# Moving the weight buffers by 96 bytes against the activations, and two split transfers joined

## The chip, the cores and the metric

The kernel runs on one core of a Trainium2 chip. The metric is the device time of one execution in microseconds (us), the median of three runs. One further execution was recorded by the hardware profiler; all rows below come from it. The engines are named as the profile names them: PE (TensorE, matrix multiplication), PEld (the loading of PE's stationary operand, which overlaps PE), DVE (VectorE), ACT (ScalarE), POOL (GpSimd) and SP (SyncE, which here only issues transfers). SPq and ACTq are the issues of transfers from SP and ACT.

## What is computed

One decoder layer for 256 tokens of width 1024, in float32: two token mixers side by side (attention with 8 heads, and a causal pooling mixer), each gated, then a feed-forward part with a causal convolution of width 3. Cut to what matters here:

```python
h = rmsnorm(x, norm_mix_g)
q, k, v, u_pool, gate_logits = split(h @ w_in)       # 1024 x 4096
attn = attention(rotary(rmsnorm(q)), rotary(rmsnorm(k)), v)
pooled = multiscale_pool_mixer(u_pool, w_pool, pool_scale)
gates = sigmoid(gate_logits + b_gate)
x = x + (gates[0] * (attn @ w_branch_attn) + gates[1] * (pooled @ w_branch_pool)) @ w_out
up = causal_depthwise_conv(rmsnorm(x, norm_ffn_g) @ w_up, conv_w, conv_b)
gate, val = split(up)                                # 2 x 2816 columns
return x + (silu(gate) * val) @ w_down
```

## The kernel before

Everything is kept transposed: channels on the 128 partitions, the 256 tokens along the row. Every product is made of three passes of PE in the type fp32r: each operand is cut into a high part (ACT copies it into fp32r: `high`, L80) and a low part (DVE subtracts the high part from the original: `low`, L84), and `mm3` (L92 to L94) adds high x high, high x low and low x high into one PSUM bank. Each of those passes first loads a stationary operand of 128x128 and then streams a moving operand. From the pooling input on (`feature_tile`, `branch`, `tile_part`, `down`), the weights are the stationary operand and 256 columns of activations move. In the stage of q, k and v (`project`, L283) it is the other way round: the activations are stationary and 512 columns of weights move.

Weights come in blocks of 128x2048 through three pools of four buffers each: `raw` (as loaded, by `load`, L121, from SP's queue), `whi` and `wlo` (high and low parts). In a partition's row of SBUF the order is: the small tiles of the pool `const`, then `raw`, `whi`, `wlo`, then the pool `act` with the activations, whose first tile is `xq` (the input x and the weights of q, interleaved by blocks of 128 channels), then `xhi`, `xlo` and the later activations. In the built program `raw`, `whi` and `wlo` start at bytes 24000, 56768 and 89536 of the row, `xq` at 122304 and `xhi` at 146912. Buffers and steps inside them are multiples of 512 bytes, so, modulo 512, all weight operands of PE stand at 448 and all activations of the dense stages at 480.

The order on each engine is the order of the program. SP issues the blocks of `xq` (L190 to L199: two of 128 channels each, then three of 256), the first weights of k, the table `par` of vectors (L202), and then a weight block each time a buffer comes free. The first block of `xq` goes out in two pieces: x of that block and the norm weights from SP (L196), the weights of q from ACT (L195). The first matmul needs `xhi` of block 0 (DVE, L226) and the high part of q's weights (ACT, L80). At the end eight output tiles are added to x by DVE (L703) and sent out, seven by SP (L705); the eighth goes in two halves of 64 partitions, one from SP and one from ACT (L707).

Of the kernel before, what the change touches and what calls it, by code (L numbers as in the profile page):

```python
# [8 lines left out]
F32 = mybir.dt.float32  # L9
# [5 lines left out]
P = 128  # L15
S = 256
NT = S // P
D = 1024
KD = D // P
H = 8  # L20
DH = 64
AW = H * DH
# [30 lines left out]
FFN_AHEAD = 6  # L53
KREADY = 0
FIRST = 2
XCUTS = (1, 2, 4, 6, 8)


@with_exitstack
def hybrid_layer_kernel(ctx: ExitStack, tc: tile.TileContext, xq_d, par_d, wkv_d, wpg_d,  # L60
                        wpool_d, wba_d, wbp_d, wout_d, wup_d, wdn_d, out_d):
    nc = tc.nc

    const = ctx.enter_context(tc.tile_pool(name="const", bufs=1))
# [3 lines left out]
    act = ctx.enter_context(tc.tile_pool(name="act", bufs=1))  # L68
# [109 lines left out]
    nc.vector.memset(ones, 1.0)  # L178


    xq_all = act.tile([P, KD + KD * (S + AW)], F32, name="xq")
    gmix = xq_all[:, 0:KD]
    xq = xq_all[:, KD:].rearrange("p (k c) -> p k c", c=S + AW)
    xT = xq[:, :, 0:S]
# [5 lines left out]
    cut = 0  # L190
    for k in XCUTS:
        end = KD + k * (S + AW)
        if k == 1:

            nc.scalar.dma_start(out=xq_all[:, KD + S:end], in_=xq_d[:, KD + S:end])  # L195
            nc.sync.dma_start(out=xq_all[:, 0:KD + S], in_=xq_d[:, 0:KD + S])  # L196
        else:
            nc.sync.dma_start(out=xq_all[:, cut:end], in_=xq_d[:, cut:end])
        cut = end  # L199
    nc.scalar.activation(scrap, ones[:, 0:1], AF.Copy)  # L200
    load(2)
# [8 lines left out]

    ident = const.tile([P, P], F32, name="ident")
    make_identity(nc, ident)
    mhalf = const.tile([P, H], F32, name="mhalf")
    nc.gpsimd.memset(mhalf, -0.5)
    mask = const.tile([P, 3, P], F32, name="mask")
# [215 lines left out]
    def scores(hp):  # L431
        ps = ps2.tile([P, 2, 512], F32, tag="ps2", name=f"ps_s{hp}")
        for j in range(2):
            rows = slice(j * DH, (j + 1) * DH)
            nc.tensor.matmul(ps[:, j, P:3 * P], qT[rows, hp, P:S], kT[rows, hp, :], start=True, stop=True)
            nc.tensor.matmul(ps[:, j, 0:P], qT[rows, hp, 0:P], kT[rows, hp, 0:P], start=True, stop=True)
        sm = tmp.tile([P, 2, 3 * P], F32, tag="big", bufs=4, name=f"sm{hp}")
        nc.vector.tensor_tensor(sm, ps[:, :, 0:3 * P],
                                mask.rearrange("p a b -> p (a b)")[:, None, :].to_broadcast([P, 2, 3 * P]), ALU.add)
        mx = tmp.tile([P, 2, 2], F32, tag="mx", name=f"mx{hp}")  # L440
        for t in (1, 0):
            nc.vector.tensor_reduce(mx[:, t, :], sm[:, :, TOK[t]], axis=AX.X, op=ALU.max)
        nc.vector.tensor_scalar(mx, mx, -(DH ** -0.5), None, op0=ALU.mult)
        sums = tmp.tile([P, 2, 2], F32, tag="sums", name=f"sums{hp}")
        for j in range(2):
            for t in (1, 0):
                nc.scalar.activation(sm[:, j, TOK[t]], sm[:, j, TOK[t]], AF.Exp, bias=mx[:, t, j:j + 1],
                                     scale=DH ** -0.5, accum_out=sums[:, t, j:j + 1])
        rs = tmp.tile([P, 2, 2], F32, tag="rs", name=f"rs{hp}")
        nc.vector.reciprocal(rs, sums)  # L450
        for t in (1, 0):
            n = TOK[t].stop - TOK[t].start
            nc.gpsimd.tensor_tensor(sm[:, :, TOK[t]], sm[:, :, TOK[t]],
                                    rs[:, t, :, None].to_broadcast([P, 2, n]), ALU.mult)
        later(4, weigh, hp, sm)
# [46 lines left out]
    for n in range(2 * KD):  # L502
        if n >= FIRST and (n - FIRST) % 4 == 0:
            scores((n - FIRST) // 4)
        if n == 10:
# [126 lines left out]
    def down(i, ms):  # L632
        if i % 2 == 0 and i // 2 not in wd:
            wd[i // 2] = chunk("dn")
        hi, lo = wd[i // 2]
        for m in ms:
            sl = slice((i % 2) * D + m * P, (i % 2) * D + (m + 1) * P)
            o = acc[m // 2][:, (m % 2) * S:(m % 2 + 1) * S]
            first = i == 0 and m % 2 == 0
            nc.tensor.matmul(o, hi[:, sl], acch[i], start=first, stop=False, skip_group_check=True)  # L640
            nc.tensor.matmul(o, hi[:, sl], accl[i], start=False, stop=False, skip_group_check=True)  # L641
            nc.tensor.matmul(o, lo[:, sl], acch[i], start=False, stop=i == KF - 1, skip_group_check=True)  # L642
        if i % 2 == 1 and len(ms) == KD:
            spent.add(next(c for c in his if his[c] is hi))
# [54 lines left out]
    for m in (0, 2, 4, 6, 1, 3, 5, 7):  # L699
        for i in (KF - 2, KF - 1):  # L700
            down(i, (m,))
        o = acc[m // 2][:, (m % 2) * S:(m % 2 + 1) * S]
        nc.vector.tensor_tensor(xT[:, m, :], o, xT[:, m, :], ALU.add)  # L703
        if m < 7:
            nc.sync.dma_start(out=out_d[:, m, :], in_=xT[:, m, :])  # L705
    for q, rows in ((nc.sync, slice(0, P // 2)), (nc.scalar, slice(P // 2, P))):
        q.dma_start(out=out_d[rows, 7, :], in_=xT[rows, 7, :])  # L707


    last = {}  # L710
# [70 lines left out]
```

## Time and profile before

| | us |
|---|---|
| median of three runs | 347.86 (347.85 to 348.05) |
| the profiled execution, whole | 347.8 |
| its span, first to last instruction | 346.0 |
| PE busy in the span | 340.3 (98%) |
| PEld, DVE, ACT, POOL busy | 329.3, 259.3, 198.1, 89.4 |
| mean rate of all transfers | 181 GB/s |

Busy times of matmuls overlap: a matmul is recorded from its start to the modelled end of its result, while the next has already begun. The pace of PE is therefore read from the distance between starts, not from the duration of one. The granted clock of PE is 1.00 of its 2.4 GHz level in every slice of the span but the last, after the last matmul.

### The profile page before, as it was taken

The numbers are of one execution on the slowest core, as the hardware profiler recorded it, in microseconds if no ns is written. First come the engines' busy times: TensorE is split into PE (matmuls) and PEld (weight loads), VectorE is DVE, ScalarE is ACT, GpSimd is POOL, SyncE is SP. The second block draws the span as 40 slices with busy tenths as digits, with TensorE's granted clock in tenths as the row PEclk, the third lists the DMA queues.
The fourth block names the chain that finished last, engine by engine and source line by source line (L and its number), as shares of the span: only waits on it lengthen the run. The fifth ranks groups of instructions, "written<-read, shape, count | busy, mean of one in ns | idle before, by whom it ended". The sixth has DMA issues, their size and how long they took to land.

```text
span 346.0 us, 6726 instructions
## 1 busy us (share of the span) xinstructions
PE 340.3 (98%) x2736; PEld 329.3 (95%) x2736; DVE 259.3 (75%) x411; ACT 198.1 (57%) x319; POOL 89.4 (26%) x103
## 2 busy tenths in 40 slices
PE   8999999999999999999999999999999999999995
PEld 7887899999999999999999999999999999999995
DVE  4969889787587585798699977777777777768633
ACT  4956534634748944776467755555556464646420
POOL 1007991112202034123142212121212121221230
PEclk9999999999999999999999999999999999999999
DMA  7985642365272560574257557364646455641003
GB/s 273 421 333 211 217 168 108 150 214 213 86 265 90 230 215 30 172 275 170 116 197 268 183 206 243 122 244 131 236 137 228 145 223 168 209 180 54 0 2 121
DMA packets 10414, 62.76 MB, mean 181 GB/s; under 512 B 1168, under 2 KB 2448, under 8 KB 3472
## 3 DMA queue, kind: packets, MB, share of 16 engines
q1 hardware_dynamic: 10160, 62.01, 49.9%
q8 instruction: 21, 0.34, 0.4%
q10 hardware_dynamic: 224, 0.33, 0.3%
q14 instruction: 9, 0.07, 0.1%
HBM read 61.29 MB, written 1.05 MB: 180 GB/s over the span
## 4 chain that ended last, share of the span: by engine, by line
PE 90%; DMA 5%; DVE 3%; ACT 1%; issue 0%; POOL 0%; SPq 0%; ACTq 0%
PE ps_up L94 12%; PE ps_up L92 12%; PE ps_up L93 12%; PE ps_d L642 6%; PE ps_d L641 6%; PE ps_d L640 6%; PE ps_g L92 5%; PE ps_g L94 4%; PE ps_g L93 4%; DMA raw_k<-in_wkv 3%; PE ps_v L283 3%; PE ps_out L92 2%; PE ps_out L94 2%; PE ps_out L93 2%; PE ps_bp L92 1%; DMA xq<-in_xq 1%
## 5 line engine op out<-in xcount | busy, mean ns | idle before, releaser
L92 PE MATMUL ps_up<-hhi,hi_up 128*128 128x256 f32 x352 | 98.5, 280 | 0.0
L94 PE MATMUL ps_up<-hhi,lo_up 128*128 128x256 f32 x352 | 98.4, 279 | 0.0
L93 PE MATMUL ps_up<-hlo,hi_up 128*128 128x256 f32 x352 | 98.3, 279 | 0.0
L94 PEld LDWEIGHTS ps_up<-hhi,lo_up 128*128 128x128 f32 x352 | 66.2, 188 | 0.2 <-DVE lo_up L84 0.2
L92 PEld LDWEIGHTS ps_up<-hhi,hi_up 128*128 128x128 f32 x352 | 66.2, 188 | 0.0
L93 PEld LDWEIGHTS ps_up<-hlo,hi_up 128*128 128x128 f32 x352 | 66.2, 188 | 0.0
L84 DVE TENSOR_TENSOR lo_up<-raw_up,hi_up 128x1024 fp32r<-128x1024 f32 x44 | 54.5, 1242 | 6.1 <-ACT hi_up L80 6.1
L641 PE MATMUL ps_d<-al,hi_dn 128*128 128x256 f32 x176 | 49.1, 279 | 0.0
L640 PE MATMUL ps_d<-ah,hi_dn 128*128 128x256 f32 x176 | 49.1, 279 | 0.0
L642 PE MATMUL ps_d<-ah,lo_dn 128*128 128x256 f32 x176 | 49.1, 279 | 0.0
L623 POOL TENSOR_TENSOR c_v<-c_g,c_v 128x256 f32<-128x256 f32 x22 | 16.2, 736 | 121.4 <-DVE c_v L606 121.4
L80 ACT ACTIVATE hi_up<-raw_up 128x1024 fp32r<-128x1024 f32 x44 | 44.9, 1044 | 0.0
L92 PE MATMUL ps_g<-xhi,hi_g 128*128 128x256 f32 x128 | 36.5, 285 | 0.0
L93 PE MATMUL ps_g<-xlo,hi_g 128*128 128x256 f32 x128 | 35.7, 279 | 0.0
L94 PE MATMUL ps_g<-xhi,lo_g 128*128 128x256 f32 x128 | 35.7, 279 | 0.0
L80 ACT ACTIVATE ah<-c_v 128x256 fp32r<-128x256 f32 x22 | 9.2, 419 | 45.7 <-POOL c_v L623 45.7
L641 PEld LDWEIGHTS ps_d<-al,hi_dn 128*128 128x128 f32 x176 | 33.1, 188 | 0.0
L642 PEld LDWEIGHTS ps_d<-ah,lo_dn 128*128 128x128 f32 x176 | 33.1, 188 | 0.0
L640 PEld LDWEIGHTS ps_d<-ah,hi_dn 128*128 128x128 f32 x176 | 33.1, 188 | 0.0
L611 DVE TENSOR_TENSOR u_v<-ps_up,R 128x256 f32<-128x256 f32 x22 | 9.3, 422 | 25.7 <-PE ps_up L94 25.6
L84 DVE TENSOR_TENSOR lo_dn<-raw_dn,hi_dn 128x1024 fp32r<-128x1024 f32 x22 | 27.8, 1264 | 0.4 <-ACT hi_dn L80 0.4
L647 POOL TENSOR_TENSOR al<-c_v,ah 128x256 fp32r<-128x256 f32 x22 | 22.8, 1038 | 11.6 <-ACT ah L80 11.6
(182 smaller groups left out, 806.7 us busy)
## 6 DMA issues: line engine op xcount, KB each, us to landing
raw_up<-in_wup SPq DMA_DIRECT2D x22, 1024.0 KB, 4.8
raw_dn<-in_wdn SPq DMA_DIRECT2D x11, 1024.0 KB, 4.7
raw_g<-in_wpg SPq DMA_DIRECT2D x8, 1024.0 KB, 4.8
raw_o<-in_wout SPq DMA_DIRECT2D x4, 1024.0 KB, 4.7
xq<-in_xq SPq DMA_DIRECT2D x3, 768.0 KB, 7.4
raw_v<-in_wkv SPq DMA_DIRECT2D x2, 1024.0 KB, 14.0
raw_p<-in_wpg SPq DMA_DIRECT2D x2, 1024.0 KB, 6.2
raw_bp<-in_wbp SPq DMA_DIRECT2D x2, 1024.0 KB, 4.7
```

The costliest lines, as they stand in the source:

```text
L80: nc.scalar.activation(hi, src, AF.Copy, scale=scale)
L84: nc.vector.tensor_tensor(lo, src, hi.bitcast(F32), ALU.subtract)
L92: nc.tensor.matmul(out, sh, mh, start=start, stop=False, **kw)
L93: nc.tensor.matmul(out, sh, ml, start=False, stop=False, **kw)
L94: nc.tensor.matmul(out, sl, mh, start=False, stop=stop, **kw)
L283: nc.tensor.matmul(pt[t], sx[:, k, t * P:(t + 1) * P], wx[:, sl], start=k == 0 and sx is xhi and wx is hi, stop=k == KD - 1 and wx is lo)
L611: nc.vector.tensor_tensor(u, ps[:, 0:S], R2, ALU.mult)
L623: nc.gpsimd.tensor_tensor(uc[1], g[1], uc[1], ALU.mult)
L640: nc.tensor.matmul(o, hi[:, sl], acch[i], start=first, stop=False, skip_group_check=True)
L641: nc.tensor.matmul(o, hi[:, sl], accl[i], start=False, stop=False, skip_group_check=True)
L642: nc.tensor.matmul(o, lo[:, sl], acch[i], start=False, stop=i == KF - 1, skip_group_check=True)
L647: nc.gpsimd.tensor_tensor(accl[i], act_i, acch[i].bitcast(F32), ALU.subtract)
```

## The change

Three edits. They shift the line numbers: by two down as far as the code of `xq`, by one to three up behind it (`high` is L82, `load` L123, the output transfers L703).

- A tile `home` of 24 floats is placed among the small tiles; POOL writes one column of it. Everything behind it moves by 96 bytes, so the three weight pools now start at 24096, 56864 and 89632: 32 modulo 512.
- `xq` gets 104 unused floats at its start (416 bytes). The content of `xq` and all activations behind it are thus 512 bytes further than before, unchanged modulo 512: `xhi` starts at 147424, that is 480. Activations minus weights was 32 bytes modulo 512 and is now 448.
- The first block of `xq` is one transfer of 128x776 from SP, and the eighth output tile one of 128x256 from SP. ACT issues no transfer any more.

```diff
+HOME = 24
+LEAD = 104
...
-    xq_all = act.tile([P, KD + KD * (S + AW)], F32, name="xq")
+    xq_all = act.tile([P, LEAD + KD + KD * (S + AW)], F32, name="xq")[:, LEAD:]
...
-        if k == 1:
-
-            nc.scalar.dma_start(out=xq_all[:, KD + S:end], in_=xq_d[:, KD + S:end])
-            nc.sync.dma_start(out=xq_all[:, 0:KD + S], in_=xq_d[:, 0:KD + S])
-        else:
-            nc.sync.dma_start(out=xq_all[:, cut:end], in_=xq_d[:, cut:end])
+        nc.sync.dma_start(out=xq_all[:, cut:end], in_=xq_d[:, cut:end])
...
+    home = const.tile([P, HOME], F32, name="home")
+    nc.gpsimd.memset(home[:, 0:1], 0.0)
...
-        if m < 7:
-            nc.sync.dma_start(out=out_d[:, m, :], in_=xT[:, m, :])
-    for q, rows in ((nc.sync, slice(0, P // 2)), (nc.scalar, slice(P // 2, P))):
-        q.dma_start(out=out_d[rows, 7, :], in_=xT[rows, 7, :])
+        nc.sync.dma_start(out=out_d[:, m, :], in_=xT[:, m, :])
```

Names and numbers of lines apart, the instructions of PE and DVE stand in the same order as before; POOL has the one memset more. The other differences are at three places. Names in brackets are what an instruction waits for: DMAHW is the completion of an earlier transfer (eight counters, used in turn), DVE and Activation are engines. First, the start of SP's queue, before:

```order
L776 UNCONDITIONAL_BRANCH [waits barrier_Pool_Activation_PE_DVE_SP_release]
L196 DMA xq<-in_xq 128x264
L198 DMA xq<-in_xq 128x768
L198 DMA xq<-in_xq 128x1536 x3
L121 DMA raw_k_93<-in_wkv 128x1024 x2
L202 DMA par<-in_par 128x396 [waits DMAHW0_49]
L121 DMA raw_k_97<-in_wkv 128x2048 [waits DMAHW1_49]
L121 DMA raw_v_99<-in_wkv 128x2048 [waits DMAHW2_49]
```

and after:

```order
L772 UNCONDITIONAL_BRANCH [waits barrier_Pool_Activation_PE_DVE_SP_release]
L195 DMA xq<-in_xq 128x776
L195 DMA xq<-in_xq 128x768
L195 DMA xq<-in_xq 128x1536 x3
L123 DMA raw_k_92<-in_wkv 128x1024 x2
L199 DMA par<-in_par 128x396
L123 DMA raw_k_96<-in_wkv 128x2048 [waits DMAHW0_49]
L123 DMA raw_v_98<-in_wkv 128x2048 [waits DMAHW1_49]
```

The first transfer has grown from 264 to 776 columns, SP still issues five for `xq`, and `par` no longer waits for the first transfer; the block behind it does. Second, the start of ACT, before:

```order
L776 UNCONDITIONAL_BRANCH
L195 DMA xq<-in_xq 128x512
L200 ACT_TABLE_LOAD
L200 ACTIVATE scrap<-ones 128x1
L80 ACTIVATE hi_q_129<-xq 128x512
L80 ACTIVATE xhi<-xq 128x256
```

and after:

```order
L772 UNCONDITIONAL_BRANCH
L197 ACT_TABLE_LOAD
L197 ACTIVATE scrap<-ones 128x1
L82 ACTIVATE hi_q_130<-xq 128x512
L82 ACTIVATE xhi<-xq 128x256
```

ACT begins with its table load, one issue earlier than before. Third, the end of SP's queue, before:

```order
L705 DMA out_T<-xq 128x256 [waits DVE_49] x4
L705 DMA out_T<-xq 128x256 [waits DMAHW4_49,DVE_49]
L705 DMA out_T<-xq 128x256 [waits DMAHW5_49,DVE_49]
L705 DMA out_T<-xq 128x256 [waits DMAHW6_49,DVE_49]
L707 DMA out_T<-xq 64x256 [waits DMAHW0_49,DVE_49]
```

and after:

```order
L703 DMA out_T<-xq 128x256 [waits DVE_49] x4
L703 DMA out_T<-xq 128x256 [waits DMAHW3_49,DVE_49]
L703 DMA out_T<-xq 128x256 [waits DMAHW4_49,DVE_49]
L703 DMA out_T<-xq 128x256 [waits DMAHW5_49,DVE_49]
L703 DMA out_T<-xq 128x256 [waits DMAHW6_49,DVE_49]
```

The eighth tile is one whole transfer of the same form as the seven before it.

## Rows read from the trace of the kernel before

**Rows 1.** The page: busy time of each engine; shares of the chain that ended last

```profile
PE 340.3 (98%) x2736; PEld 329.3 (95%) x2736; DVE 259.3 (75%) x411; ACT 198.1 (57%) x319; POOL 89.4 (26%) x103
...
PE 90%; DMA 5%; DVE 3%; ACT 1%; issue 0%; POOL 0%; SPq 0%; ACTq 0%
```

**Rows 2.** Stretches: length, busy us of PE, PEld, DVE, ACT, POOL, clock, DMA share, GB/s

```profile
5.27:17.22 11.95, 11.95 (x48) 9.54 (x49) 10.34 (x17) 9.84 (x18) 0.00 (x0) 1.00 1.02 418
...
165.10:342.00 176.90, 176.87 (x1514) 176.62 (x1512) 130.43 (x199) 97.07 (x146) 39.03 (x44) 1.00 0.47 164
342.00:346.00 4.00, 0.19 (x2) 0.00 (x0) 0.42 (x1) 0.00 (x0) 0.00 (x0) 0.83 0.34 98
```

**Rows 3.** The same view for the instructions of one tile: first ps_out, then ps_k

```profile
133.60:156.30 22.70, 22.56 (x192) 22.40 (x192) 2.90 (x7) 1.00 0.53 182
```
```profile
17.20:23.00 5.80, 5.76 (x24) 4.32 (x23) 0.00 (x0) 0.00 (x0) 1.00 1.00 418
```

**Rows 4.** Groups of matmuls by line and shape (busy, mean ns); a timeline row

```profile
L92 PE MATMUL ps_up<-hhi,hi_up 128*128 128x256 f32 x352 | 98.5, 280 | 0.0
...
L319 PE MATMUL ps_tq<-ident,qg_q 128*128 128x128 f32 x8 | 1.0, 272 | 0.0
```
```profile
L254 PE MATMUL ps_n<-diag,ones 128*128 128x256 f32 x4 | 1.2, 378 | 0.0
...
L94 PE MATMUL ps_m<-poolh,lo_pool 128*128 128x256 f32 x4 | 1.1, 278 | 0.0
```
```profile
46.59 1.03 PE L319 MATMUL ps_tq<-ident,qg_q 128*128 128x128 f32 x8
```

**Rows 5.** Single matmuls (mean ns), and timeline rows of the loads behind them

```profile
L283 PE MATMUL ps_v<-hi_v,xhi 128*128 128x512 f32 x1 | 0.4, 397 | 0.0
L283 PE MATMUL ps_k<-lo_k,xhi 128*128 128x512 f32 x1 | 0.4, 395 | 0.0
```
```profile
29.30 0.40 PE L283 MATMUL ps_v<-hi_v,xhi 128*128 128x512 f32 x1
...
29.90 0.19 PEld L283 LDWEIGHTS ps_v<-hi_v,xhi 128*128 128x128 f32 x1 [0.65 <-PE ps_k L283]
```
```profile
L94 PE MATMUL ps_g<-xhi,lo_g 128*128 128x256 f32 x1 | 0.3, 274 | 0.0
```
```profile
L94 PE MATMUL ps_g<-xhi,lo_g 128*128 128x256 f32 x1 | 0.3, 280 | 0.0
```
```profile
L642 PE MATMUL ps_d<-ah,lo_dn 128*128 128x256 f32 x1 | 0.3, 278 | 0.0
```

**Rows 6.** The front: timeline rows, and one row of transfer sizes with us to landing

```profile
0.74 0.41 ACTq L195 DMA_DIRECT2D xq<-in_xq  x1
...
4.40 0.35 DVE L226 TENSOR_SCALAR xhi<-xq 128x256 fp32r<-128x256 f32 x1 [1.82 <-DMA xq<-in_xq]
...
4.58 0.63 ACT L80 ACTIVATE hi_q<-xq 128x512 fp32r<-128x512 f32 x1 [1.91 <-DMA xq<-in_xq]
...
7.63 0.51 ACT L80 ACTIVATE xhi<-xq 128x256 fp32r<-128x256 f32 x1 [0.81 <-DMA xq<-in_xq]
```
```profile
8.71 0.30 PEld L283 LDWEIGHTS ps_q<-hi_q,xhi 128*128 128x128 f32 x2 [0.18 <-ACT hi_q L80]
```
```profile
xq<-in_xq SPq DMA_DIRECT2D x1, 384.0 KB, 4.5
```

**Rows 7.** The end: timeline rows; sizes of the output transfers and us to landing

```profile
342.68 0.55 SPq L707 DMA_DIRECT2D out_T<-xq  x1
342.68 0.56 ACTq L707 DMA_DIRECT2D out_T<-xq  x1
```
```profile
out_T<-xq SPq DMA_DIRECT2D x7, 128.0 KB, 1.9
...
out_T<-xq SPq DMA_DIRECT2D x1, 64.0 KB, 2.2
out_T<-xq ACTq DMA_DIRECT2D x1, 64.0 KB, 2.5
```

**Rows 8.** Timeline: a memset of POOL

```profile
1.25 0.10 POOL L214 MEMSET mhalf<- 128x8 f32 x1
```

## The prediction

> **What bounds the kernel now.** I read the page first: PE is busy 98% of the span, and the chain that ended last is PE for 90% [rows 1]. A busy PE need not be a PE at its best, so the next view is the busy time by stretches. From 165 us to the last matmul PE has 0.03 us of idle time in 176.9, while DVE is busy 74% and ACT 55% of it, and the transfers use 0.47 of their engines [rows 2]. Nothing that the other engines do is waited for there. The time of this kernel is therefore the number of matmuls times the distance between their starts, and the one thing in the change that can move it by much is that distance.
>
> The distance is read from the stretch in which one tile name has PE to itself. The 192 matmuls of ps_out (256 columns each) fill 22.56 us [rows 3]; the last one's own length is 0.28, so 191 distances are 22.28 us, or 116.65 ns each. The 24 of ps_k (512 columns) fill 5.76 us, so 23 distances in 5.36 us are 233 ns, just twice as much: 0.455 ns a column in both. The groups with 256 columns in the three passes run from x352 for ps_up to x4 for ps_m [rows 4]; there are 24 of these groups, and counts of 352, 176, 128, 64, three times 32 and 4, each three times, add up to 2460 matmuls. At 116.65 ns they are 287 us, 83% of the span.
>
> **Is there slack in that distance?** Plain float32 work on the same PE gives a measure. Eight transposes of 128 columns take 1.03 us, one lasts 272 ns [rows 4], so they start 109 ns apart; and the plain float32 matmul of 256 columns lasts 378 ns, 106 more for 128 columns more, so 0.83 ns a column at the same granted clock. If the type fp32r ran at exactly twice that rate, 256 columns would take 106 to 109 ns. It takes 7.65 ns longer than the 109. That excess, 7.65 ns x 2460 = 18.8 us, is all that a better placing of operands could win in these stages, and the question of this prediction is whether it comes from the load of the next weights meeting the stream of the activations in SBUF, which the placing would change, or from the stream itself, which it would not.
>
> The trace can answer in part, because a few matmuls stream with no load under them. At 29.30 us a matmul of 512 columns runs while the next load starts only at 29.90; it lasts 397 ns, its neighbour with a load under it 395 [rows 5]. Were the load the cause, the lone one should be some 17 ns shorter. Seven matmuls of 256 columns are alone in the same way (before the scores and the values of attention, at one wait for weights, and the last of all); they last 274 to 280 ns, of which a 274, a 280 and the last with 278 are shown [rows 5], against 278 to 280 in the groups. Their mean of 277 is about 2 ns short, not 7.65. And an interplay with one load of 128 columns per matmul should cost the same whether 256 or 512 columns stream, but the excess doubles with the columns. So the rows say that the stream itself is this slow. The ends of matmuls are modelled in this profile, which is why I do not take it as settled.
>
> The Trainium skill has two rules here that point in different directions. "TensorE: Matmul & The Clock Gate", section "Step-by-step: what each phase is for", says that PE reads the moving operand and the weights through two independent ports, so that loading the next weights takes nothing from the running matmul; by that rule the sum below keeps its pace term at zero, and the lone matmul of 397 ns agrees. The same page's "Back-to-back issue gap" gives a distance of columns divided by 2.4 plus 2.5 ns, which would be 109 ns; the trace disagrees by the 7.65 ns above, and its result is a rival below.
>
> **The change part by part.**
>
> *Weights moved by 96 bytes.* The edit adds no instruction on PE. In the dense stages the moving operand stays at 480 modulo 512 and the stationary one goes from 448 to 32; in the q, k, v stage the moving weights go from 448 to 32. That is 2460 distances that may change, between -7.65 ns (the excess vanishes, -18.8 us) and +7.65 ns (a second excess of the same size, +18.8 us). I take 0, since the nearest rows, the lone matmuls, show the stream's length unchanged when the load is gone altogether. DVE and ACT read and write the same buffers with the same mutual distances, except against the activations; I cost them at nothing, since they have a quarter of the dense stretch idle; without that cover each 1% on DVE there would be 1.3 us.
>
> *The memset of `home`.* One more memset of POOL, 0.10 us by its neighbour [rows 8]. What POOL then hands on late is needed by DVE, which sits idle for 1.82 us before 4.40 [rows 6]; cost 0, and 0.10 us without that cover.
>
> *The first block in one transfer.* ACT's issue of 0.41 us disappears ahead of a wait of 1.91 us for data [rows 6]: nothing. The block of 388 KB can land as early as its smaller piece did, for DVE's start at 4.40, 0.2 us ahead of ACT's start at 4.58; or as late as the second block did after its issue, 4.5 us [rows 6], that is 0.74 + 4.5 = 5.24, 0.7 us later. Behind it ACT has three copies of 0.5 to 0.63 us before it waits 0.81 us for the third block at 7.63, and PE waits for what follows, at 8.71 [rows 6]. So even 0.7 us is given back by then: ACT would be through at about 7.0, and the third block is not late since the bytes ahead of it are the same. I take 0, with -0.2 and +0.7 as ends. In SP's queue `par` loses its wait for the first transfer and the next block of k gets it; the issues behind them, v's blocks, wait for landings that stay where they are. The transfer engines are full there (share 1.02 in [rows 2]), so an issue some tenths earlier or later finds a queue of work in front of it.
>
> *The last output in one transfer.* The halves are issued at 342.68; the later one lands 2.5 us after that and the seven whole tiles took 1.9 each [rows 7]. The whole tile goes the same way as those seven and nothing is queued behind it, so the end comes 0.6 us earlier. Ends: -0.6, and 0 if the last transfer takes as long as the later half.
>
> *Sum.* The profiled execution took 347.8 us, span 346.0 and 1.8 around it, 0.06 under the median. From the median: 347.86 + 0 + 0 + 0 - 0.6 = **347.3 us**. With its own ends (the pace uncertain by 0.1 ns or 0.25 us, front -0.2 to +0.7, tail -0.6 to 0) this case reaches from 346.8 to 348.5.
>
> **The rivals.**
>
> *The load does cost the stream its 7.65 ns, and the new distance of 448 bytes avoids it.* For it: fp32r is slower than twice the rate of plain float32, and the lone matmuls are 2 ns shorter. Against it: 397 ns with no load, and the excess that grows with the columns. In full it gives 347.3 - 18.8 = 328.5 us; with only the 2 ns of the lone matmuls 4.9 us, so 342.4. DVE could follow, its 74% would become 79%. The Trainium skill's formula for the gap, cited above, would have the full one.
>
> *The new distance makes load and stream meet* (the slower side). The place is every matmul of the dense stages: weights at 32 and activations at 480 now have the same remainder modulo 64, where before one was a multiple of 64 and the other was not. If that adds an excess of the same 7.65 ns, 366.1 us. It decides from 0.5 ns a matmul on, since 0.5 x 2460 = 1.2 us eats the tail's 0.6 and another 0.6. Against it: with nothing loaded under it the stream is just as long, so today's excess is no meeting of this kind, and the rows show none that could grow.
>
> *The joined transfers save nothing* (the change does not do what it says): without the tail's gain, 347.9 us. It is the upper half of the forecast's own range.
>
> **How the numbers follow.** The unchanged pace gets 0.60, the pace that gains 0.26 (half of that near 328.5, the rest up to 346.5), the pace that loses 0.14. A measurement of this kernel can tell about 0.2%, 0.7 us, from no change. Inside the first case a third ends below 347.16 and hardly anything above 348.56: 0.21 faster, 0.37 the same, 0.02 slower. Together: faster 0.26 + 0.21 = 0.47, the same 0.37, slower 0.14 + 0.02 = 0.16. The range takes in the first case and almost all of the second, 328.0 to 348.5, and leaves out the third; the likeliest case's own range is 346.8 to 348.5.
>
> **What would show it.** In the profile after, the 192 matmuls of ps_out should fill 22.5 to 22.6 us and the 24 of ps_k 5.76; 20.9 us for ps_out would be the full gain of the first rival, over 22.7 the second. The lone matmul of ps_v should last as long as its neighbours. The last output should land 1.9 us after its issue, with one row in place of two. The first matmul may start between 5.1 and 5.9 us, but the copy that waits for the third block should still start near 7.6. The prediction is wrong in its main step if the distance of 116.65 ns moves by more than 0.3 ns.

## The result, and the profile after

The changed kernel takes 342.81 us (median), the kernel before 347.87 beside it: a ratio of 0.9852, 95% interval 0.9833 to 0.9871. One of its four executions took 348.86 us, in a slower state, and is in the median (342.67 without it) but not in the ratio; no trace of it was kept, so what was slow in it is open. The change gains 5.1 us, or 1.5%; forecast were 347.3 us, with 328.0 to 348.5 as the range. So the time lies in the range, and on the side (faster) that had the largest chance, but it is not the forecast case that came true: the distance between matmuls, which the prediction left alone, has moved.

The page of the profile after, busy time and shares of the chain that ended last:

```profile
PE 335.4 (98%) x2736; PEld 324.6 (95%) x2736; DVE 259.9 (76%) x411; ACT 198.1 (58%) x319; POOL 87.9 (26%) x104
...
PE 85%; DVE 6%; DMA 4%; ACT 2%; SPq 1%; issue 1%; POOL 1%; POOLq 0%; ACTq 0%
```

Against [rows 1], PE has 4.9 us less of busy time with the same 2736 matmuls, and the other engines' work is as it was. The span went from 346.0 to 341.1 us, by the same 4.9. That they are equal is chance: the end is shorter without PE, and PE has new waits of about the same length. Where the gain came from is seen by cutting both spans at the same places of the program: start of ps_u, of ps_out, of the feed-forward part behind the product with `diag`, end of the matmuls. The columns are the stretch, its length, and busy time of PE, PEld, DVE, ACT, POOL, then clock, DMA share, GB/s. After:

```profile
40.70:133.20 92.50, 92.40 (x789) 89.28 (x789) 72.19 (x128) 55.30 (x105) 26.86 (x28) 1.00 0.48 174
133.20:165.25 32.05, 32.05 (x271) 31.86 (x271) 24.79 (x35) 20.68 (x33) 8.57 (x11) 1.00 0.50 173
165.25:337.70 172.45, 171.90 (x1514) 171.62 (x1512) 130.52 (x199) 97.09 (x146) 37.84 (x44) 1.00 0.47 168
337.70:341.20 3.50, 0.15 (x2) 0.00 (x0) 0.42 (x1) 0.00 (x0) 0.00 (x0) 0.97 0.34 112
```

The kernel before, cut at the same places:

```profile
40.95:133.60 92.65, 92.55 (x789) 89.42 (x788) 71.67 (x127) 55.32 (x105) 26.65 (x28) 1.00 0.48 172
133.60:165.10 31.50, 31.50 (x271) 31.48 (x270) 24.52 (x36) 20.68 (x33) 8.90 (x11) 1.00 0.51 177
165.10:341.95 176.85, 176.82 (x1514) 176.59 (x1512) 130.42 (x199) 97.07 (x146) 39.03 (x44) 1.00 0.47 164
341.95:346.00 4.05, 0.24 (x3) 0.04 (x1) 0.43 (x2) 0.00 (x0) 0.00 (x0) 0.83 0.34 97
```

The front gives 0.25 us, the attention part 0.15, the end 0.55; the middle stretch loses 0.55, and the long stretch of the feed-forward part gives 4.40. Together 4.8 of the 4.9. With equal matmul counts and the clock at 1.00 throughout, two of these stretches moved in opposite directions: that cannot be a clock, nor one new distance.

The next view is the one of [rows 3], the instructions of one tile name alone: ps_out, then ps_k, then the last 96 matmuls of ps_d, all of after, and at last those 96 of before.

```profile
120.00:160.00 40.00, 22.78 (x192) 22.68 (x192) 3.31 (x8) 1.00 0.49 170
```
```profile
17.00:22.80 5.80, 5.66 (x24) 4.32 (x23) 0.00 (x0) 0.00 (x0) 1.00 1.02 425
```
```profile
326.70:337.95 11.25, 11.04 (x96) 10.95 (x96) 3.03 (x8) 1.00 0.18 61
```
```profile
330.70:342.30 11.60, 11.36 (x96) 11.27 (x96) 3.04 (x8) 1.00 0.18 62
```

By the same sum as in the prediction, the busy time without the last matmul's own length (0.28, for 512 columns 0.39) over one less than the count: ps_out went from 116.65 to 117.8 ns, ps_d from 116.6 to 113.3, and ps_k (512 columns) from 233 to 229. The changed kernel has **two paces**, 117.8 and 113.3 ns, for the same operand places. From the starts of the single matmuls the change between the two is seen here only where the dense work is interrupted by another product: 113.3 behind the scores (ps_s) and behind the last transposes (ps_p, 114.7 us), 117.8 behind the values (ps_o), and 113.3 from 165.3 us, behind the product with `diag`, to the end. The middle stretch has 264 matmuls of the three passes, all at 117.8: 1.1 ns each are 0.3 us of the 0.55 that it lost, and a load that waits for DVE's `hlo` has 0.2 more, in the page's groups of after:

```profile
L95 PEld LDWEIGHTS ps_up<-hlo,hi_up 128*128 128x128 f32 x352 | 66.1, 188 | 0.2 <-DVE hlo L88 0.2
```

The feed-forward stretch holds 1512 matmuls; 3.33 ns each are 5.0 us. It gave 4.40, since DVE now comes late once, in the timeline of after:

```profile
184.11 0.38 PE L96 MATMUL ps_up<-hhi,lo_up 128*128 128x256 f32 x1 [0.55 <-DVE lo_up L86]
```

The end is the one that was forecast, a single row of eight whole tiles in the view of the transfers (KB, us to landing), against the three rows of [rows 7]; under it the first block's:

```profile
out_T<-xq SPq DMA_DIRECT2D x8, 128.0 KB, 1.9
...
xq<-in_xq SPq DMA_DIRECT2D x1, 388.0 KB, 3.6
```

The front, timeline of after (ACT's first copy, the first matmuls, the copy that waits for the third block):

```profile
4.33 0.63 ACT L82 ACTIVATE hi_q<-xq 128x512 fp32r<-128x512 f32 x1 [2.11 <-DMA xq<-in_xq]
...
5.02 1.22 PE L282 MATMUL ps_q<-hi_q,xhi 128*128 128x512 f32 x2 [0.18 <-ACT hi_q L82]
...
7.58 0.51 ACT L82 ACTIVATE xhi<-xq 128x256 fp32r<-128x256 f32 x1 [0.88 <-DMA xq<-in_xq]
```

ACT starts 0.25 us earlier than in [rows 6] and meets the third block at 7.58 in place of 7.63, as said: what the front gains is mostly waited away there.

### The profile page after: what moved, and what is told of

The parts are those of the page before. It is cut to its first block, busy times and chain, and to the rows that moved or that the text cites. A ratio compares the mean times of both kernels' runs of the same rounds, so it can differ in the third digit from the quotient of the medians.

```text
span 341.1 us, 6723 instructions
## 1 busy us (share of the span) xinstructions
PE 335.4 (98%) x2736; PEld 324.6 (95%) x2736; DVE 259.9 (76%) x411; ACT 198.1 (58%) x319; POOL 87.9 (26%) x104
## 4 chain that ended last, share of the span: by engine, by line
PE 85%; DVE 6%; DMA 4%; ACT 2%; SPq 1%; issue 1%; POOL 1%; POOLq 0%; ACTq 0%
PE ps_up L95 10%; PE ps_up L96 10%; PE ps_up L94 10%; PE ps_d L640 6%; PE ps_d L639 6%; PE ps_d L641 6%; PE ps_g L94 5%; PE ps_g L95 4%; PE ps_g L96 4%; DMA raw_k<-in_wkv 4%; PE ps_v L282 3%; PE ps_out L95 2%; PE ps_out L94 2%; PE ps_out L96 2%; PE ps_bp L94 1%; PE ps_ba L95 1%
## 5 line engine op out<-in xcount | busy, mean ns | idle before, releaser
L96 PE MATMUL ps_up<-hhi,lo_up 128*128 128x256 f32 x352 | 97.4, 277 | 0.6 <-DVE lo_up L86 0.6
L622 POOL TENSOR_TENSOR c_v<-c_g,c_v 128x256 f32<-128x256 f32 x22 | 16.2, 738 | 118.5 <-DVE c_v L605 118.5
L82 ACT ACTIVATE hi_up<-raw_up 128x1024 fp32r<-128x1024 f32 x44 | 45.0, 1046 | 0.0
L82 ACT ACTIVATE ah<-c_v 128x256 fp32r<-128x256 f32 x22 | 9.2, 418 | 45.8 <-POOL c_v L622 45.8
L610 DVE TENSOR_TENSOR u_v<-ps_up,R 128x256 f32<-128x256 f32 x22 | 9.3, 421 | 22.7 <-PE ps_up L96 22.7
L94 PEld LDWEIGHTS ps_g<-xhi,hi_g 128*128 128x128 f32 x128 | 24.3, 190 | 0.9 <-issue 0.3
```

What stands on the lines that cost most here:

```text
L82: nc.scalar.activation(hi, src, AF.Copy, scale=scale)
L94: nc.tensor.matmul(out, sh, mh, start=start, stop=False, **kw)
L96: nc.tensor.matmul(out, sl, mh, start=False, stop=stop, **kw)
L610: nc.vector.tensor_tensor(u, ps[:, 0:S], R2, ALU.mult)
L622: nc.gpsimd.tensor_tensor(uc[1], g[1], uc[1], ALU.mult)
```

## The experiments

**Theory A**: the distance between the addresses of a matmul's two operands in SBUF sets its pace, through some interplay of the two reads. **Rival**: padding just moves buffers, and which pace a stage gets falls by chance at each interruption (theory C), or the joined transfers give the time. Where a run has other rivals, its expectation says so. A pace below is the mean distance between the starts of matmuls of one burst in the trace, the first four distances left out; the rows shown beside it carry it as busy time.

### The two parts of the change, each alone

The kernel before with the two paddings, transfers left split:

```
+HOME = 24
+LEAD = 104
...
-    xq_all = act.tile([P, KD + KD * (S + AW)], F32, name="xq")
+    xq_all = act.tile([P, LEAD + KD + KD * (S + AW)], F32, name="xq")[:, LEAD:]
...
+    home = const.tile([P, HOME], F32, name="home")
+    nc.gpsimd.memset(home[:, 0:1], 0.0)
```

> The kernel before with the two paddings alone (home of 24 floats, 104 unused floats ahead of xq); both transfers stay split. Theory A (the gain of 5.1 us is the pace of PE, and the joined last transfer is worth 0.6): 342.8 + 0.6 = 343.4 us, with stretches of 113.3 ns a matmul as in the changed kernel; in an execution that stays at its longer pace of 117.8 ns in the feed-forward stage, some 349.5. Theory B (the pace changed for a reason tied to the transfers at the start): about 347.9, all stretches at 116.65 ns.

Measured: 343.41 us, ratio 0.9863 (0.9831 to 0.9894). The same two paces stand in the same stages, but for two short stretches: the first run of ps_u (48 matmuls) is at 113.7 in place of 117.8, and the last 22 matmuls of ps_up before 161 us, behind a wait for `hlo`, at 114 in place of 117.8. So the place does not fix which of the two paces a stage gets.

The kernel before with the joined transfers, no padding:

```
-            nc.scalar.dma_start(out=xq_all[:, KD + S:end], in_=xq_d[:, KD + S:end])
-            nc.sync.dma_start(out=xq_all[:, 0:KD + S], in_=xq_d[:, 0:KD + S])
+        nc.sync.dma_start(out=xq_all[:, cut:end], in_=xq_d[:, cut:end])
...
-    for q, rows in ((nc.sync, slice(0, P // 2)), (nc.scalar, slice(P // 2, P))):
-        q.dma_start(out=out_d[rows, 7, :], in_=xT[rows, 7, :])
+        nc.sync.dma_start(out=out_d[:, m, :], in_=xT[:, m, :])
```

> The kernel before with the two transfers joined alone (first block of xq and eighth output tile from SP), no padding. Theory A: the pace stays at 116.65 ns everywhere, the last transfer lands 1.9 us after its issue in place of 2.5, 347.87 - 0.6 = 347.3 us. Theory B: stretches at 113.3 ns, about 343.

Measured: 347.27 us, ratio 0.9979 (0.9961 to 0.9997), 0.6 us below the 347.88 beside it. So the change is two changes that add: 4.5 us by the padding, 0.6 by the transfers. The second is the prediction's term to the tenth.

### Is it the distance? A map

A kernel of bursts alone: 24 matmuls of 128x256 in three passes, as the dense stages have them, the weights shifted in steps of 32 bytes against the activations, in eight rounds: one without anything between the bursts, seven with another product there, of six kinds (the second argument is the shift of the stationary operand in floats).

```
ps = burst("abcdefghijklmnop"[i], 8 * i)
```

> A measuring kernel that leaves the layer out: bursts of 24 fp32r matmuls (256 columns, three passes over eight steps of 512 or 1024 bytes, as in the dense stages) with the stationary operand placed 0, 32, 64, ... 480 bytes modulo 512 behind the moving one (tiles ps_a to ps_p), each of the 16 places after seven kinds of separating instruction. Placed 480 behind (ps_p) is the kernel before, 64 behind (ps_c) the changed one. Theory A (the load of the next weights meets the stream; the distance modulo 512 decides the pace): ps_p 116.7 ns, ps_c 113.3 or 117.8 depending on what came ahead, other places other paces, possibly down to 109. Theory C (the distance is without effect, an execution falls into one of several paces by chance): the same mixture of 113.3, 116.7 and 117.8 at all 16 places.

Measured, ns by how far the weights stand behind the activations (the kernel before stands at 480 or 224, the changed one at 64):

| bytes | 0 | 32 | 64 | 96 | 128 | 160 | 192 | 224 |
|---|---|---|---|---|---|---|---|---|
| pace | 119.6-120.0 | 118.2-118.4 | 113.3-113.4 (6 of 8), 117.7 | 117.2-120.0 | 118.2-120.0 | 119.8-120.2 | 117.7-117.8, once 113.3 | 116.6-117.9 |
| + 256 | 119.6-120.0 | 118.2-118.4 | 113.3-113.6 (5 of 8), 117.8 | 117.2-118.8 | 118.2-118.8 | 119.8-120.2 | 117.7-117.8, once 113.3 | 116.6-117.8 |

Rows of the measuring kernel (stretch, length, busy of PE, clock, DMA): ps_a (0 bytes) after two products in row groups and after two in column groups, ps_c (64 bytes) after two in row groups and after one of one column, and ps_p (480) after two in row groups:

```profile
126.48:129.88 3.40, 3.12 (x24) 1.00 0.00 0
181.48:184.88 3.40, 3.13 (x24) 1.00 0.00 0
```
```profile
133.41:136.69 3.28, 3.00 (x24) 1.00 0.00 0
...
288.87:292.21 3.34, 3.08 (x24) 1.00 0.00 0
```
```profile
178.12:181.46 3.34, 3.06 (x24) 1.00 0.00 0
```

The same 24 matmuls at the same clock, with no transfers, keep PE busy for 3.00, 3.06 or 3.12 us by the place alone (0.1 us of each is the start of the burst). The places of both kernels give their kernels' paces: 480 has 116.6 to 116.8 in six rounds (and 117.8 in two), 64 has 113.3 or 117.7. Theory C falls as it stands: most places keep their order over the eight rounds. What is left of it is that some places, 64 bytes above all, have two paces or more, and an interruption picks one. The pattern repeats after **256 bytes**, not after the 512 of the change's own description.

The same with other shapes: the activations shifted in place of the weights, 512 columns, loads of 64 and 32 columns, the same addresses in every pass, and shifts of 4, 8 and 16 bytes.

```
tests = [("mva", 0, 32), ("mvb", 0, 64), ("mvc", 0, 96)]
tests += [("wide" + "abcdefgh"[i], 16 * i, 0, 512) for i in range(8)]
tests += [("half" + "abcd"[i], 32 * i, 0, 256, 64) for i in range(4)]
tests += [("quart" + "abcd"[i], 32 * i, 0, 256, 32) for i in range(4)]
```

> A measuring kernel that leaves the layer out, as m1_offsets, but varying the form, after four kinds of separating instruction: the moving operand shifted by 128, 256, 384 bytes in place of the stationary one (ps_mva to ps_mvc); 512 columns moving with the stationary one 0, 64, ... 448 bytes behind (ps_widea to ps_wideh); stationary operands of 64 and 32 columns (ps_half, ps_quart); the same two addresses in every matmul (ps_fixa, ps_fixb with 448 behind); places 4, 8 and 16 bytes behind (ps_finea to ps_finec). Theory A: a shift of the moving operand by x gives the pace of a shift of the stationary one by -x; smaller loads cost the stream less, half and quart nearer to 109 ns than 128 columns at the same place; wide between 216 and 234 ns and depending on the place. Theory D (the stream itself is slow, as the prediction had it): half and quart at 116.7 as well, wide at 233 throughout.

Measured: shifting the activations by 128, 256 or 384 bytes gives the paces of the weights shifted the other way (118.5 to 120.1, 119.6 to 119.9, 118.5 to 120.1), so moving either operand does the same. With a period of 256 bytes these three cannot tell a shift of one operand from the opposite shift; that the relative place counts, and not the place of one operand, is shown by the run that moves both together (r3_together, below). The same two addresses in every matmul gave 119.7 to 120.0 at 0 bytes and 117.7 to 117.8 at 448. 512 columns have the same period with levels of their own: 226.9 to 228.0 at 0 and 256 bytes, 233.2 to 233.5 at 64 and 320, 231.9 to 233.6 at 128 and 384, 228.7 to 229.1 at 192 and 448. The activations of ps_k, its stationary operand, stand 448 behind the weights in the changed kernel, and its 229 ns are that level; the 32 of before (233 ns) was not among the places. Loads of 64 columns gave 113.3 to 116.8 and of 32 columns 113.3 to 120.0: a smaller load does not end the excess, but it changes the pace of a place. At 0 bytes 64 columns have 113.3 to 113.9 where 128 have 119.6 to 120.0, at 128 bytes 116.6 to 116.8 where 128 have mostly 118.2 to 118.8, so theory A's half about smaller loads held for 64 columns. Shifts of 4, 8, 16 bytes gave 118.0, 115.8 and up to 120.0, so 32 bytes is too coarse a step for the map.

Hence a finer one, 64 places in steps of 4 bytes:

```
ps = burst("abcdefgh"[i // 8] + "abcdefgh"[i % 8], i)
```

> A measuring kernel: the layer is left out. Products of 24 fp32r matmuls (128x256, stationary 128 columns), the stationary operand in steps of 4 bytes, 0 to 252, behind the moving one: the first letter of a tile's name counts 32 bytes, the second 4 bytes (ps_ca is 64 bytes, the place of the changed kernel). Each place three times: after a plain fp32 product with the matrix of ones, after two products in row groups, after a transpose. Theory A (the distance of the two operands sets the pace): each place has a pace of its own between 113 and 120 ns, the same after all three separators or one of two; ps_aa 119.8, ps_ca 113.3. Theory B (only whole steps of 32 bytes count): the eight names with one first letter agree within 0.5 ns. Theory C (chance at each interruption): no order over the places.

Measured: in 42 of 64 places the three repeats agree within 0.6 ns, so theory A holds for these, and in the others the separator has a part; theory B falls: inside one step of 32 bytes paces run from 113.3 to 120. Over all places they run from 113.3 to 120.7, with one burst at 122.2. Below 115 ns in some repeat are 52, 64, 76, 88 and 168, 180, 192, 204 bytes: two rows of four places, 12 bytes apart within a row. Only two of the eight were short in all three repeats, 76 bytes (113.3, 114.2, 113.4) and 88 (113.8 each). The changed kernel's 64 was at 113.6, 113.6 and 117.8.

### Back in the kernel: the map's places

`HOME` and `LEAD` alone are changed, their sum kept at 128 except in the last of the three.

```
r1_zero      HOME = 8,  LEAD = 120    (0 bytes behind)
r2_period    HOME = 88, LEAD = 40     (64 + 256 behind)
r3_together  HOME = 24, LEAD = 0      (weights moved as in the change, activations with them)
```

> The changed kernel with the weights at the activations' own place, modulo 512 (HOME 8, LEAD 120: distance 0 in place of 448). Theory A, from the measuring kernel (distance 0: 119.6 to 120.0 ns where the place before has 116.7 and the changed one 113.3 or 117.8): 2460 matmuls at 3.1 ns more than before, less the 0.6 us of the end, is 354.9 us, between 353 and 357. The theory that any padding helps by moving the buffers: 343.

> The changed kernel with the distance 192 in place of 448 (HOME 88, LEAD 40). Theory A with a period of 256 bytes: the same paces as the changed kernel, 113.3 or 117.8 ns, and 342 to 347 us by which of the two each stage takes. Theory with a period of 512 bytes: another pace, outside this range or with other paces than these two.

> The changed kernel with LEAD 0 in place of 104: the weights still stand 96 bytes further than in the kernel before, and the activations now go 96 bytes further with them, so that the distance is 32 as before. Theory A (the distance alone sets the pace): 116.65 ns as before and the end's 0.6 us less, 347.3 us, as with the joined transfers alone. Theory that the place of the weights counts: 342.8 as the changed kernel, or any other time.

Measured: 354.67 us (ratio 1.0190, 1.0165 to 1.0214), 342.81 (0.9848, 0.9828 to 0.9868), 347.69 (0.9986, 0.9972 to 1.0000). The row of ps_out, columns as above, in that order:

```profile
120.00:160.00 40.00, 23.20 (x192) 23.11 (x192) 2.91 (x7) 1.00 0.47 174
```
```profile
120.00:160.00 40.00, 22.78 (x192) 22.68 (x192) 3.31 (x8) 1.00 0.48 175
```
```profile
120.00:160.00 40.00, 22.56 (x192) 22.47 (x192) 3.32 (x8) 1.00 0.51 170
```

120.0, 117.8 and 116.65 ns. The same kind of padding makes this kernel 2% slower or 1.5% faster, and leaves it where it was when both operands move together. A distance longer by 256 bytes has the changed kernel's time. The third came out 0.4 us above its 347.3. Its end saves what the others' do, and its trace shows where the 0.4 went: from the start of ps_out to the feed-forward part it takes 31.94 us, against 31.49 in the kernel before, with one load of PE waiting for DVE (us, times, longest):

```profile
PEld ps_up L95 <- DVE hlo L88: 0.4, 1, 0.4
```

So `hlo` comes late by the padding alone, at the old pace. That run also shows a second pace at the place of before: its first 158 matmuls of the feed-forward part are at 117.8, and behind a delay of 0.15 us the rest are at 116.7.

### A version that beats both

In the changed kernel each weight buffer is made 256 bytes wider and used from a column inside it, so that the weights stand a few bytes further.

```
+SHIFT = 6
...
-  his[c] = whi_p.tile([P, CH], F32R, tag="whi", name=f"hi_{order[c][0]}{c}")
+  his[c] = whi_p.tile([P, CH + 64], F32R, tag="whi", name=f"hi_{order[c][0]}{c}")[:, SHIFT:SHIFT + CH]
```

`los[c]` is made in the same way; SHIFT is 3 in the second version.

> The changed kernel with every weight buffer 64 columns wider and used from its sixth column on: the weights stand 24 bytes further, 88 behind the activations modulo 256 in place of 64. Theory A (the distance sets the pace) with the map of the measuring kernel (ps_cg 113.8 ns after all three separators): one pace of about 113.8 ns in every dense stage, no stage at 117.8, so (116.65 - 113.8) x 2460 = 7.0 us and the 0.6 us of the end less than before: 340.3 us, between 339.5 and 341.5. If the two paces of the changed kernel come from the interruptions and not from the place: 342.8 as the changed kernel.

> The same with the third column (12 bytes further, 76 behind): Theory A with the map (ps_cd 113.3, 114.2, 113.4 ns): 113.3 to 114.2 ns in every dense stage, 339.0 to 341.3 us, likeliest 339.5. If the two paces of the changed kernel come from the interruptions and not from the place: 342.8.

Measured: 342.46 us for 88 bytes (ratio 0.9837, 0.9821 to 0.9854), 341.24 for 76 (0.9811, 0.9787 to 0.9835). Against the changed kernel's 0.9852 (0.9833 to 0.9871) the first is no clear gain; the second is the faster one, by an interval that just touches. The 96 matmuls of ps_ba, at 88 and at 76 bytes:

```profile
119.00:136.00 17.00, 11.36 (x96) 1.00 0.41 150
```
```profile
119.00:136.00 17.00, 11.04 (x96) 1.00 0.37 126
```

11.04 us are 113.3 ns, the pace of the feed-forward part, which 76 bytes has in every dense stage: none is at 117.8 any more. At 88 bytes the first run of ps_u, most of the attention part and ps_out stand at 116.7, though the map showed 113.8 three times; three repeats were too few to see a second pace, and that expectation failed. At 76 bytes the range held and its likeliest value of 339.5 did not: with PE 2.5 us ahead of the kernel before by ps_out's end, DVE is late with its splits. Waits of PE, then of PEld, of this kernel (us, times, longest; the front's are left out, which ends 0.3 us earlier than before in spite of them):

```profile
PE ps_up L96 <- DVE hlo L89: 0.7, 1, 0.7
...
PE ps_up L97 <- DVE lo_up L87: 0.6, 1, 0.6
```
```profile
PEld ps_out L96 <- DVE ml L87: 0.5, 2, 0.3
```

These add up to 1.8, about the 1.7 between 341.24 and 339.5. A faster PE meets the next engine where a few of its inputs were just in time; of the wait for `hlo`, some 0.4 is there at the old pace too (r3_together).

### What is it in the reads? Size of load and of stream

Bursts at eight places, with `cols` columns of weights under `n` moving columns:

```
for name, cols, n in (("two", 2, 256), ("eight", 8, 256), ("full", P, 256),
                      ("short", P, 128), ("mid", P, 192), ("long", P, 384)):
    for i in range(8):
        separate(kind, ps)
        ps = burst(name + "abcdefgh"[i], 8 * i, cols=cols, n=n)
```

> A measuring kernel: the layer is left out. Products of 24 fp32r matmuls at eight places of the stationary operand (a to h: 0, 32, ... 224 bytes behind the moving one), each after a plain fp32 product and after a transpose. Loads of 2, 8 and 128 columns under 256 moving columns (ps_two, ps_eight, ps_full), and 128, 192 and 384 moving columns over loads of 128 (ps_short, ps_mid, ps_long). Theory L (the pace above 109 ns is the meeting of load and stream): with loads of 2 columns every place falls to about 109 ns, with 8 columns within 1 ns of that, and ps_full shows 113.3 to 120 as before; the excess over 109 ns at 256 columns stays about the same number of ns at 192 and 384 columns. Theory S (the stream alone has it, by its place): ps_two and ps_eight spread over 113 to 120 ns like ps_full, and the excess grows with the moving columns.

Measured: with loads of 2 columns, bursts at 113.3, 116.7 and 120.0 ns; with 8 columns the same three; with 128 columns 113.4 to 120.0. With 128 or 192 moving columns 111.4 to 112.0 at every place; with 384 from 173.2 to 176.7. Rows of the loads and of one kind of matmul (ns: least, median, most), ps_two at 0 and at 160 bytes,

```profile
L119 PEld LDWEIGHTS ps_twoa<-mh,wh x16: 82/83/84, 29.0 to 195.6; 128*2 128x2 f32 x16
L119 PE MATMUL ps_twoa<-mh,wh x16: 276/276/467, 29.0 to 195.7; 128*2 128x256 f32 x16
```
```profile
L119 PEld LDWEIGHTS ps_twof<-mh,wh x16: 83/83/85, 45.1 to 210.4; 128*2 128x2 f32 x16
L119 PE MATMUL ps_twof<-mh,wh x16: 282/283/468, 45.1 to 210.5; 128*2 128x256 f32 x16
```

and loads of 128 columns (ps_full) at 0 bytes:

```profile
L119 PEld LDWEIGHTS ps_fulla<-mh,wh x16: 188/192/192, 80.7 to 243.0; 128*128 128x128 f32 x16
L119 PE MATMUL ps_fulla<-mh,wh x16: 283/283/468, 80.7 to 243.2; 128*128 128x256 f32 x16
```

Theory L falls in its simple form: with a load of two columns, 83 ns long, no place comes near 109 ns, and at 160 bytes a matmul has the 283 of a full load. Theory S holds for the spread, and fails in two points: at 128 and 192 columns the place has no effect, and at one place the load changes the pace. At 0 bytes loads of 2, 8 and 128 columns have 113.3 to 113.8, 116.7 to 116.8 and 119.7 to 120.0. With a load of two columns, 113.3 and 120.0 still alternate by place and by separator. The mechanism stays open: the relative place, the number of weights and the interruption ahead all have a part in the pace (in this kernel, whose dense loads all have 128 columns, the place and the interruption), and no form of the type fp32r at 256 columns went below 113.3.

The Trainium skill, "TensorE: Matmul & The Clock Gate", section "Step-by-step: what each phase is for", has two independent read ports, so that a load takes nothing from the running matmul. The map above disagrees, as far as the relative place of the two operands sets the pace (113.3 to 120.2 ns at one clock). That it would be bandwidth which the load takes is not shown either, since loads of two columns have bursts at 120.0 as full ones do. The 109 ns by the formula in the same page's "Back-to-back issue gap", which the page gives there for a matmul by itself, was reached by no fp32r burst of 256 columns here.

## Why the prediction was right in its range and wrong in its main step

- **What bounds the kernel**: right. PE alone, its distance times its count; every run of the kernel here follows its paces but for waits of a microsecond or two.
- **Weights moved by 96 bytes**: wrong. The term was put at 0, with a range of -18.8 to +18.8 us; it measured -4.5 (347.88 to 343.41 with the paddings alone). By the prediction's own criterion, 0.3 ns, the step failed: 113.3 and 117.8 stand in place of 116.65. That the time still lies in the range is owed to a range wide enough for the first rival, and not to the step. The failing step is the reading of the lone matmuls [rows 5]. A matmul's length in this profile is its distance and about 163 ns: 280 at 116.7, 281 at 117.8, 276 at 113.3, 283 at 120.0, and 272 at the 109 of the transposes. So the seven lone ones, 274 to 280, already held lengths that belong to 111 to 117 ns; I took their mean as a nearly unchanged stream, when their spread was the news. And from "no load under it, no shorter" I concluded that no placing could matter. The changed kernel shows that the lone matmul could not tell: in ps_v it lasts 397 ns as before, as the prediction's sign for it wanted, while its neighbours' distance fell from 233 to 229.
- **The excess that doubles with the columns**: the second reason against a change did not hold either. In the kernel before, the two were at different places, since the operands change their roles: the stationary one stands 480 behind the moving one at 256 columns and 32 behind at 512. Over the map 256 and 512 columns have each their own levels (at 0 bytes 119.8 but 227.5), so the doubling was an accident of these two places. The 17 ns that a lone matmul of 512 columns was to be shorter are 15 by the prediction's own rows (233 less twice 109).
- **Memset, first block**: right as terms of the sum; with the joined transfers alone ps_u starts no earlier (41.12 against 40.97 us), and only the end is shorter. The first matmul starts at 5.02 us, just under the 5.1 to 5.9 given, and the third block's copy at 7.58 against "near 7.6".
- **Last output**: right, -0.6 forecast, -0.61 by the joined transfers alone, 1.9 us from issue to landing.
- **Rival 1** (the excess can be avoided): it is the case that came true, in its smaller form. Its part price, 342.4, is 0.4 from the 342.81 measured, and that is luck, for the reason is another one: not 2 ns everywhere, but 3.3 ns gained in the feed-forward part, about 1.1 lost in most of the rest, and 0.6 waited for DVE. Its mechanism, a load meeting a stream, is not shown.
- **Rival 2** (the new distance makes it worse): it exists, at another place. At distance 0 the kernel takes 354.67, against the 366.1 that a full second excess would have given. In the changed kernel it shows as the 117.8 ns of ps_out, 0.22 us for its 192 matmuls; their 22.78 us are over the 22.7 that the prediction named as this rival's sign, while the kernel as a whole got faster.
- **Rival 3** (the joined transfers save nothing): fell.
- **The chances**: the pace that gains got 0.26. With an excess of 7.65 ns in sight and one place out of many known, the rows could not tell what a new place does; equal shares for a gain, a loss and no change would have been closer to what they showed. Two small sums are off and decide nothing: the first case's own ends add up to 348.8 and not 348.5, and the full gain would have left ps_out at 21.1 us and not 20.9.

## What to carry to other kernels

Where a stage is nothing but matmuls behind each other, work out the distance between their starts from a stretch with one tile name, for each stage, and compare it with the cheapest distance seen anywhere on the same engine; a steady excess of some percent is worth a sweep over the relative place of the two operands, in steps finer than 32 bytes, and in the kernel itself, since a short burst can miss a second pace. Moving one pool by an unused column is then a change like any other: it should be tried at several places, not argued at one. And once PE is faster, look for the first wait on another engine: here, with 3 ns gained on each matmul, two splits that had been in time cost PE 1.3 us of waiting, about 0.4 of it not by the faster pace.

## What the runs showed of the hardware that was not expected

- For fp32r matmuls of 256 columns the relative place of weights and activations in SBUF sets which distances between starts occur: 113.3 to 120.7 ns at granted clock 1.00 (one burst at 122.2), the same after 256 bytes, with fine structure below 32 bytes. For 512 columns it is 226.9 to 233.6.
- One place can have two paces (113.3 and 117.8 at 64 bytes), kept over as many as 1512 matmuls. Where the pace changed, the stream had been interrupted: by other products, or by a wait (117.8 to 114 behind the wait for `hlo` with the paddings alone).
- With loads of 2 or 8 columns the paces are 113.3, 116.7 and 120.0 ns, steps of 3.33 ns, which is 8 periods of 2.4 GHz. The number of weights changes which of them a place has (at 0 bytes 113.3, 116.7 and 120.0 for 2, 8 and 128 columns). With 128 and 192 moving columns over loads of 128 there is one pace, 111.4 to 112.0, at every place.
